# A hybrid diffusion backbone on one core: solve transfers issued by ScalarE, modulation steps paused ahead of the second half's pairs, and six more column pairs in seven products

## The chip, the cores and the metric

The kernel runs on one core of a Trainium2 chip. The time is that of one execution on the device in microseconds (us), as a median over runs. Five engines work side by side, each through its own list of instructions in order: TensorE (PE in the profile; PEld is its weight load), VectorE (DVE), ScalarE (ACT), GpSimd (POOL) and SyncE (SP), which here only issues transfers. A transfer's issue stands in the list of the engine that issues it, and waits there for what it needs.

## The reference, cut to what matters

Two streams of 256 tokens of width 1024, context and latent, go through two layers with the same weights: a SwiGLU FFN at half weight, a mixer, and another FFN. Each of the three parts is modulated by vectors (`mx`, `mc`) that are products of a condition with a large matrix. In the second layer only the latent stream leaves the mixer.

```python
def swiglu(h, w_gu, w_down):
    gate, up = jnp.split(h @ w_gu, 2, axis=-1)
    return (jax.nn.silu(gate) * up) @ w_down
...
    gc = jnp.cumsum(g, axis=-1)                      # gated DeltaNet, chunks of 64
    a = jnp.where(strict, jnp.einsum("bhnid,bhnjd->bhnij", kb, k) * decay, 0.0)
    t = lax.linalg.triangular_solve(eye + a, eye, left_side=True, lower=True, unit_diagonal=True)
    attn = jnp.where(incl, jnp.einsum("bhnid,bhnjd->bhnij", q, k) * decay, 0.0)
...
    for layer in range(DEPTH):
        mx = jnp.split((silu_c @ ada_w[layer] + ada_b[layer])[:, None, :], N_MOD, axis=-1)
        mc = jnp.split((silu_cc @ ada_w[layer] + ada_b[layer])[:, None, :], N_MOD, axis=-1)
        x = x + 0.5 * mx[2] * swiglu(modulate(rmsnorm(x, ...), mx[0], mx[1]), ffn1_wgu, ffn1_wd)
        # cx the same with mc
        fx, gx = mixer_features(hx @ w_in[layer], ...)  # retention q k v, DeltaNet q k v, beta, g, gates
        (ret_c, dn_c), (ret_x, dn_x) = bidirectional_mix(fc, fx, log_gamma)
        x = x + mx[5] * mixer_output(ret_x, dn_x, gx, ...)
        x = x + 0.5 * mx[8] * swiglu(modulate(rmsnorm(x, ...), mx[6], mx[7]), ffn2_wgu, ffn2_wd)
```

The FFN's hidden width is 2816, that is 22 column groups of 128 for the gate and 22 for the up half: a *pair* is a gate group and its up group.

## The kernel before, in words

**Products in three matmuls.** Both streams lie side by side as 512 columns (256 context, 256 latent). Every operand of a large product is kept as a rounded head and a rest: `wh`, `wl` for a weight tile of 128 x 128, `xh`, `xl` for the activations. One tile takes three matmuls of 512 columns, all recorded under line 394 (`mat`). Weights are streamed: SyncE loads 128 x 1024 raw tiles (`_load`, lines 427 and 432), ScalarE rounds the head (`wh`, line 382), VectorE subtracts for the rest (`wl`, line 511). With `self.plo` GpSimd takes every second rest. Four weight tiles make one `wh` and one `wl` of 128 x 512, a group; `_ensure` keeps the heads of the next five groups and the rests of the next four formed, as far as the engines come. A transfer of the next raw tile is issued when the raw buffer before it is freed.

**Pairs in seven products.** `FAST` says how many pairs of an FFN's first and second half go plain; the others of the 11 in a half go through `pairs`, Strassen's scheme over blocks of tiles and of the two streams. It takes seven products of four tiles with 256 columns, 84 matmuls of 256, where a plain pair takes 16 tiles, 48 matmuls of 512. Its weight forms are sums of raw tiles: SyncE loads two more tiles, GpSimd adds by two accumulating transfers (line 461) and two additions (line 464), and seven heads and seven rests are formed instead of four of each. The keys are (layer, FFN), with FFN 0 ahead of the mixer and 2 behind it.

**Modulation steps in the background.** The modulation vectors of all later parts (15 items of 16 steps) are formed by VectorE, one custom row of 128 x 1024 per step (line 803), each on a 512-KB raw tile that SyncE loads two steps ahead (`ada_spread`, line 778). `background` lets a step into VectorE's list whenever `self.gap` microseconds of planned TensorE work have passed; `None` stops them. `RATE` and `RATES` give the gap for plain groups, for pairs and for the down product of an FFN, `MIX_RATE` for the mixers. The first seven items must be done before layer 0's mixing ends.

**FFN.** `ffn` does two halves: 11 pairs, then the down product in eight groups of 11 tiles over this half, each group ending with `evd(m, ...)`, which adds to the residual stream (VectorE, line 388, `s<-mm,mods,s`).

**Mixer.** `run` lets a projection (`dense`) advance while other generators are placed beside it: each yields how much projection work should pass before its next instructions. In layer 0: the retention's keys, queries and values; then `ret_mix` and its gated output beside the other projections; then `dn_small` (the decay `dn_decay`, lengths `dn_len`, scales), `dn_mix` (per chunk set: `dn_prep`) and `dn_scan`. `dn_decay` transposes its 16 inputs (line 398), computes beta and g on VectorE (from line 1523), and has TensorE multiply g with constants (`mx<-g,con`). `dn_prep` forms the system of both directions: transposes of the key and query rows, products of keys and queries, VectorE rows with the decay (line 388, `s<-d,ngc,con`) and products from PSUM (line 385, `s<-mx,s`); then `prep_solve` puts the system to DRAM (`dw`), loads it again as blocks of 16 rows, solves by VectorE subtractions, puts the result to DRAM (`dx`) and loads it as matrices (`ut`). All four kinds of its transfers are issued by SyncE. There are four solves, one for each stream of each layer. The convolution of the DeltaNet's inputs is four VectorE rows of about 508 elements per tile (line 388, `s<-mm,par,s`).

## Time and profile before

| | us |
|---|---|
| median of 3 runs (lowest, highest) | 2405.55 (2404.73, 2806.76) |
| the profiled execution | 2410.67 |
| its span | 2408.9 |
| TensorE busy (matmuls) | 2331.9, 97% |
| VectorE busy | 1762.3, 73% |
| ScalarE busy | 1144.1, 47% |
| GpSimd busy | 549.3, 23% |

The mean granted clock of TensorE in the profiled execution is 0.989 of full speed, whose two levels are 2.4 and 1.2 GHz. The chain of waits that ended last runs through TensorE for 77% of the span, VectorE 12%, issue 5%, DMA 3%, ScalarE 2%. Stretches are named by their start in the profiled execution: layer 0's first FFN ends near 440, its mixer's DeltaNet part starts near 585; layer 1's solves lie near 1880 and 2060.

How to read the views: a *timeline* lists the instructions of one engine in order, with the idle time before each and the last of those it waited for in brackets; *windows* give busy time and granted clock by stretch; *waits* sum the idle time by what ended it; a row *by line* groups instructions of one line and form. For a queue (SPq) a row's duration covers several issues and what stood between them.

### The profile page before, as it was taken

The numbers are of one execution on the slowest core, as the hardware profiler recorded it, in microseconds if no ns is written. First come the engines' busy times: TensorE is split into PE (matmuls) and PEld (weight loads), VectorE is DVE, ScalarE is ACT, GpSimd is POOL, SyncE is SP. The second block draws the span as 40 slices with busy tenths as digits, with TensorE's granted clock in tenths as the row PEclk, the third lists the DMA queues.
The fourth block names the chain that finished last, engine by engine and source line by source line (L and its number), as shares of the span: only waits on it lengthen the run. The fifth ranks groups of instructions, "written<-read, shape, count | busy, mean of one in ns | idle before, by whom it ended". The sixth has DMA issues, their size and how long they took to land.

```text
span 2408.9 us, 42549 instructions
## 1 busy us (share of the span) xinstructions
PE 2331.9 (97%) x16352; PEld 2081.8 (86%) x16352; DVE 1762.3 (73%) x3134; ACT 1144.1 (47%) x2310; POOL 549.3 (23%) x512
## 2 busy tenths in 40 slices
PE   7999999999999999999999999999999899899998
PEld 5888989887788888889899889899888689889998
DVE  6888986558785646579799689899684458677554
ACT  4423545344554444365245365255355446455444
POOL 1003521022330200134144134154124232100001
PEclk9999999999999999999999999999999999999999
DMA  7657763233241414355677555676524324546553
GB/s 287 214 182 221 209 190 121 96 132 132 96 114 58 129 61 149 126 165 143 213 206 193 184 143 155 219 214 183 200 92 138 84 84 138 157 146 222 181 186 112
DMA packets 177325, 377.87 MB, mean 157 GB/s; under 512 B 49697, under 2 KB 54625, under 8 KB 177121
## 3 DMA queue, kind: packets, MB, share of 16 engines
q1 hardware_dynamic: 161184, 346.28, 43.2%
q0 software_dynamic: 13536, 24.65, 6.2%
q10 hardware_dynamic: 2400, 4.23, 0.6%
q8 instruction: 128, 2.10, 0.4%
q14 instruction: 77, 0.62, 0.1%
HBM read 364.83 MB, written 10.26 MB: 156 GB/s over the span
## 4 chain that ended last, share of the span: by engine, by line
PE 77%; DVE 12%; issue 5%; DMA 3%; ACT 2%; SPq 0%; POOL 0%; DVEq 0%; ACTq 0%; POOLq 0%
PE mm L394 66%; PE mx L394 10%; DVE wl L511 5%; DVE s L385 2%; DVE s L803 2%; DVE s L388 2%; ACT s L382 2%; DMA d<-in_adat_dram 1%; PE mx L398 1%; DMA raw<-in_w_dram 0%; ACT wh L382 0%; DVE sub L385 0%; DMA s<-gd 0%; DMA s<-in_x_dram 0%; DVE s L908 0%
## 5 line engine op out<-in xcount | busy, mean ns | idle before, releaser
L394 PE MATMUL mm<-s,wh 128*128 128x256 f32 (+1 forms) x7794 | 1788.4, 324 | 13.0 <-ACT s L382 5.7
L394 PEld LDWEIGHTS mm<-s,wh 128*128 128x128 f32 x7794 | 1295.0, 189 | 142.7 <-ACT s L382 9.0
L394 PE MATMUL mm<-s,wl 128*128 128x256 f32 (+1 forms) x3901 | 1259.0, 323 | 10.6 <-DVE wl L511 8.9
L394 PEld LDWEIGHTS mm<-s,wl 128*128 128x128 f32 x3901 | 738.0, 189 | 73.4 <-DVE wl L511 10.7
L382 ACT ACTIVATE s<-s 128x512 fp32r<-128x512 f32 (+4 forms) x564 | 291.8, 526 | 541.5 <-DVE s L385 287.7
L511 DVE TENSOR_TENSOR wl<-raw,wh 128x512 fp32r<-128x512 f32 x569 | 420.1, 754 | 110.5 <-ACT wh L382 75.5
L382 ACT ACTIVATE wh<-raw 128x512 fp32r<-128x512 f32 x628 | 381.1, 625 | 231.9 <-PE mm L394 140.8
L803 DVE CUSTOM_DVE_ANT_0 s<-d,d,par 128x1024 bf16<-128x1024 f32 x240 | 326.7, 1361 | 33.4 <-DMA d<-in_adat_dram 32.9
L511 DVE TENSOR_TENSOR wl<-s,wh 128x512 fp32r<-128x512 f32 x368 | 311.4, 858 | 21.7 <-ACT wh L382 12.2
L382 ACT ACTIVATE wh<-s 128x512 fp32r<-128x512 f32 x369 | 218.3, 622 | 55.0 <-PE mm L394 46.7
L385 DVE TENSOR_TENSOR s<-s,s 128x512 fp32r<-128x512 f32 (+3 forms) x306 | 191.7, 637 | 40.7 <-ACT s L382 36.8
L382 ACT ACTIVATE s<-mm 128x256 f32<-128x256 f32 (+2 forms) x259 | 110.2, 426 | 228.9 <-PE mm L394 228.5
L464 POOL TENSOR_TENSOR s<-s,raw 128x512 f32<-128x512 f32 x84 | 145.5, 1732 | 111.7 <-DMA raw<-in_w_dram 37.0
L394 PE MATMUL mx<-s,s 32*32 32x32 f32 (+3 forms) x1820 | 152.1, 250 | 11.3 <-DVE s L385 10.1
L394 PEld LDWEIGHTS mx<-s,s 32*32 32x32 f32 (+2 forms) x1820 | 133.6, 149 | 23.2 <-issue 11.5
L461 POOL DMA_DIRECT2D s<-in_w_dram x94 | 83.5, 984 | 277.2 <-DMA s<-in_w_dram 249.5
L908 POOL TENSOR_TENSOR s<-s,s 128x512 f32<-128x512 f32 (+1 forms) x31 | 36.1, 1164 | 435.1 <-ACT s L382 434.8
L511 POOL TENSOR_TENSOR wl<-raw,wh 128x512 fp32r<-128x512 f32 x59 | 80.4, 1363 | 234.9 <-ACT wh L382 113.3
L388 DVE SCALAR_TENSOR_TENSOR s<-mm,mods,s 128x256 f32<-128x256 f32 x132 | 58.7, 478 | 77.5 <-PE mm L394 77.4
L388 DVE SCALAR_TENSOR_TENSOR s<-mm,par,s 128x508 f32<-128x508 f32 (+3 forms) x124 | 87.4, 710 | 13.5 <-ACT s L382 11.1
L385 DVE TENSOR_TENSOR s<-s,mm 128x512 f32<-128x512 f32 (+1 forms) x88 | 54.0, 613 | 42.7 <-PE mm L394 39.5
L382 ACT ACTIVATE s<-mx 128x256 f32<-128x256 f32 (+5 forms) x113 | 50.3, 447 | 72.7 <-PE mx L394 64.3
(227 smaller groups left out, 1528.2 us busy)
## 6 DMA issues: line engine op xcount, KB each, us to landing
raw<-in_w_dram SPq DMA_DIRECT2D x319, 512.0 KB, 3.4
s<-in_w_dram SPq DMA_DIRECT2D x289, 256.0 KB, 5.5
d<-in_adat_dram SPq DMA_DIRECT2D x120, 512.0 KB, 4.7
s<-in_w_dram POOLq DMA_DIRECT2D x94, 256.0 KB, 5.9
s<-in_ada_dram SPq DMA_DIRECT2D x48, 256.0 KB, 5.8
s<-in_tab_dram SPq DMA_DIRECT2D x17, 256.0 KB, 4.5
xd<-s SPq DMA_DIRECT2D x16, 256.0 KB, 4.0
s<-gd ACTq DMA_DIRECT2D x9, 256.0 KB, 6.0
```

The lines of the kernel that those rows point to most:

```text
L382: return self.nc.scalar.activation(out, in_, f, **kw)
L385: return self.nc.vector.tensor_tensor(out, a, b, op)
L388: return self.nc.vector.scalar_tensor_tensor(out, a, s, b, op0=op0, op1=op1)
L394: return self.nc.tensor.matmul(out, lhsT, rhs, start=start, stop=stop, **kw)
L398: return self.nc.tensor.transpose(out, in_, self.ident[:n, :n])
L461: self.nc.gpsimd.dma_start(d[f], b, accum_op=ALU.add)
L464: self.nc.gpsimd.tensor_tensor(d[f], d[src[0]], self.raw[u][0][src[1]], ALU.add)
L511: eng.tensor_tensor(lo, self._src(s), hi.bitcast(F32), ALU.subtract)
L803: self.nc.vector.tensor_tensor_reduce(junk, raw, cb[st], 1.0, self.par[:, b:b + 1], ALU.mult, ALU.add, m[:, st, k:k + 1])
L908: eng.tensor_tensor(acc[:, n0:n1], acc[:, n0:n1], s[:, n0:n1], ALU.add)
```

## The change

Six things differ. `FAST` sends four more pairs of FFN (0, 0) through seven products in its first half, and one more each in (0, 2) and (1, 0). `evd` now sets the gap to `None` also in the first half of those FFNs from group 5 on, so that no step is placed beside the last two down groups; the second half's pairs set it again. `MIX_RATE` becomes 3.0 in layer 0's mixing and 4.0 in layer 1's, and has a third value, 3.6, for layer 0's output stage, which now goes through `run` and so carries steps. In layer 0 `dn_decay` leaves `dn_small` and goes beside `ret_mix`. The transfers of `prep_solve` are issued by ScalarE, with pauses 6, 6, 5 x 2, 1, 6 and 8 for 4, 6, 5 x 2, 5 and 13. In layer 1 GpSimd goes on forming every second rest through the last projections.

```diff
--- before.py
+++ after.py
@@ -61,7 +61,7 @@
 
 
 
-FAST = {(0, 0): (11, 0), (0, 2): (4, 0), (1, 0): (4, 0)}
+FAST = {(0, 0): (7, 0), (0, 2): (3, 0), (1, 0): (3, 0)}
 
 
 def _plain(l, j, half):
@@ -183,7 +183,7 @@
 
 RATE = (10.0, 7.6, 2.2)
 RATES = {(0, 0, 0): (2.8, 8.0, 2.2)}
-MIX_RATE = (2.3, 6.0)
+MIX_RATE = (3.0, 4.0, 3.6)
 
 FIRST_MODS = 7
 
@@ -1189,7 +1189,7 @@
 
             def evd(m, ps, a=n0, b=n1):
                 self.x_add(ps, m, l, gate, a, b)
-                if half == 1 and nxt and m == 3:
+                if half == 1 and nxt and m == 3 or half == 0 and fast and m == 5:
 
                     self.gap = None
                 if half == 1:
@@ -1482,7 +1482,6 @@
                                     self.ph, ALU.pow)
 
         if full:
-            yield from self.dn_decay(l)
             yield lambda: self.nkc == 4
             yield from self.dn_len(self.dk, 0, putk)
         else:
@@ -1721,8 +1720,8 @@
         nc = self.nc
         dw, dx = self.dw, self.dx
         for i, z in enumerate(st):
-            nc.sync.dma_start(dw[i].rearrange("g p n -> p g n"), z["bd"][:, 0:256].rearrange("p (g n) -> p g n", g=8))
-        yield 4.0
+            nc.scalar.dma_start(dw[i].rearrange("g p n -> p g n"), z["bd"][:, 0:256].rearrange("p (g n) -> p g n", g=8))
+        yield 6.0
         ws = self.A()
         W, X = ws[:, 0:256], ws[:, 256:512]
         tmp = self.small([128, 64], "sub", 2)
@@ -1730,7 +1729,7 @@
         part = lambda s, i, f: s[64 * i + 32 * f:64 * i + 32 * f + 32].rearrange("p (r c) -> p r c", r=16)
         for i in range(2):
             for f in range(2):
-                nc.sync.dma_start(part(W, i, f), blk(dw, i, f))
+                nc.scalar.dma_start(part(W, i, f), blk(dw, i, f))
         nc.gpsimd.memset(X, 0.0)
         nc.gpsimd.memset(X[:, 0:256:17], 1.0)
         yield 6.0
@@ -1742,17 +1741,18 @@
             self.tt(xv[:, 0:k, k:16], xv[:, 0:k, k:16], tv, ALU.subtract)
             if k % 3 == 1:
                 yield 2.0
+        yield 1.0
         for i in range(2):
             for f in range(2):
-                nc.sync.dma_start(blk(dx, i, f), part(X, i, f))
+                nc.scalar.dma_start(blk(dx, i, f), part(X, i, f))
         self.Fr(ws)
-        yield 5.0
+        yield 6.0
         for i, z in enumerate(st):
             z["ut"] = ut = self.A()
             for d in range(2):
-                nc.sync.dma_start(ut[:, d * 384:d * 384 + 128].rearrange("p (h n) -> p h n", h=4),
+                nc.scalar.dma_start(ut[:, d * 384:d * 384 + 128].rearrange("p (h n) -> p h n", h=4),
                                   dx[i][d * 4:d * 4 + 4].rearrange("h p n -> p h n"))
-        yield 13.0
+        yield 8.0
 
     def prep_inverse(self, z):
 
@@ -2045,7 +2045,8 @@
             yield from self.gate_out(self.ro, srg, full)
 
         small = self.chain(self.dn_small(l, full), self.dn_mix(l, full))
-        ret = self.chain(self.ret_mix(l, full), ret_out())
+        ret = self.ret_mix(l, full)
+        ret = self.chain(self.zip(ret, self.dn_decay(l)) if full else ret, ret_out())
 
         def d0():
             yield from self.ret_proj_k(full)
@@ -2070,7 +2071,7 @@
 
         def d2v():
             yield from self.dn_proj_v(l)
-            self.plo = False
+            self.plo = not full
 
         if full:
             self.run(d0())
@@ -2093,7 +2094,7 @@
             self.ret = self.gated
             self.run(d2(), self.dn_scan(l, full), scale=0.65)
 
-        self.deep, self.split_dbl = 2, False
+        self.deep, self.split_dbl, self.plo = 2, False, False
         self.bgmax = len(SPREAD)
 
         def d3():
@@ -2132,8 +2133,9 @@
             self.Fr(ys[m])
             y.append(self.split(g, n0, 512, 0.5, 1))
 
-        for _ in self.dense(G_K8, KD, lambda k: dn[k], n0, 512, ev):
-            pass
+        if full:
+            self.gap = MIX_RATE[2]
+        self.run(self.dense(G_K8, KD, lambda k: dn[k], n0, 512, ev))
         for a, b in dn:
             self.Fr(a, b)
         self.sq_start()
@@ -2142,9 +2144,9 @@
             self.x_add(ps, m, l, 5, a, b)
             self.sq_tile(m, a, b)
 
-        for _ in self.dense([4, 1] if full else G_WO, KD, lambda k: y[k], n0, 512, evo):
-            pass
+        self.run(self.dense([4, 1] if full else G_WO, KD, lambda k: y[k], n0, 512, evo))
         if full:
+            self.gap = None
             self.drain()
             for _ in self.tail((5, 6, 7), KD, lambda k: y[k], evo, l, 2):
                 pass
```

What the order of instructions shows at three places. First VectorE, ahead of the first second-half pair of FFN (0, 0): line 803 is a modulation step on the raw tile `d`, `wl<-raw` and `wl<-s` are rests, and line 388 the residual additions of the last two down groups. Before:

```order
L803 ISA s_659,mods<-d_1816,d_658,par 128x1024
L803 ISA mods 128x1
L511 TENSOR_TENSOR wl<-s_1616,wh 128x512
L388 SCALAR_TENSOR_TENSOR s_74<-mm,mods,s_74 128x256 x2
L803 ISA s_659,mods<-d_1859,d_657,par 128x1024
L803 ISA mods 128x1
L511 TENSOR_TENSOR wl<-s_1618,wh 128x512
L803 ISA s_659,mods<-d_1859,d_658,par 128x1024
L803 ISA mods 128x1
L511 TENSOR_TENSOR wl<-s_1770,wh 128x512
```

Of the change:

```order
L803 ISA s_659,mods<-d_1934,d_658,par 128x1024
L803 ISA mods 128x1
L511 TENSOR_TENSOR wl<-raw,wh 128x512
L388 SCALAR_TENSOR_TENSOR s_72<-mm,mods,s_72 128x256 x2
L511 TENSOR_TENSOR wl<-raw,wh 128x512 x3
L388 SCALAR_TENSOR_TENSOR s_73<-mm,mods,s_73 128x256 x2
L511 TENSOR_TENSOR wl<-s_1979,wh 128x512
L511 TENSOR_TENSOR wl<-s_1850,wh 128x512
L388 SCALAR_TENSOR_TENSOR s_74<-mm,mods,s_74 128x256 x2
L511 TENSOR_TENSOR wl<-s_1852,wh 128x512
L803 ISA s_659,mods<-d_1975,d_657,par 128x1024
L803 ISA mods 128x1
```

Before, a step stands ahead of nearly every rest, those of the pair's first forms (`wl<-s`) among them; now none stands from the residual addition of `s_72` to the third of these rests.

Then VectorE, in layer 0's `dn_prep` for the context, from the decay rows (`ngc,con`) to the last product of the system (`s<-mx,s`), which reads the PSUM buffer of the key products. Before:

```order
L388 SCALAR_TENSOR_TENSOR s_6500<-d_6452,ngc,con 128x128 x4
L511 TENSOR_TENSOR wl<-raw,wh 128x512
L388 SCALAR_TENSOR_TENSOR s_6447<-mm,par,s_6447 128x2x255
L388 SCALAR_TENSOR_TENSOR s_6447<-mm,par,s_6447 128x2x254
L388 SCALAR_TENSOR_TENSOR s_6532<-mm,par,s_6532 128x2x254
L388 SCALAR_TENSOR_TENSOR s_6532<-mm,par,s_6532 128x2x255
L385 TENSOR_TENSOR s_6578<-mx,s_6478 128x512
L385 TENSOR_TENSOR s_6582<-mx,s_6484 128x512
L511 TENSOR_TENSOR wl<-raw,wh 128x512
L388 SCALAR_TENSOR_TENSOR s_6532<-mm,par,s_6532 128x2x255
L388 SCALAR_TENSOR_TENSOR s_6532<-mm,par,s_6532 128x2x254
L385 TENSOR_TENSOR s_6607<-mx,s_6489 128x512
```

Of the change:

```order
L388 SCALAR_TENSOR_TENSOR s_6770<-mm,par,s_6770 128x2x254
L388 SCALAR_TENSOR_TENSOR s_6770<-mm,par,s_6770 128x2x255
L803 ISA s_659,mods<-d_6658,d_658,par 128x1024
L803 ISA mods 128x1
L385 TENSOR_TENSOR s_6820<-mx,s_6716 128x512
L385 TENSOR_TENSOR s_6824<-mx,s_6722 128x512
L511 TENSOR_TENSOR wl<-raw,wh 128x512
L388 SCALAR_TENSOR_TENSOR s_6770<-mm,par,s_6770 128x2x255
L388 SCALAR_TENSOR_TENSOR s_6770<-mm,par,s_6770 128x2x254
L803 ISA s_659,mods<-d_6772,d_657,par 128x1024
L803 ISA mods 128x1
L385 TENSOR_TENSOR s_6852<-mx,s_6727 128x512
```

Steps of line 803 now stand between the convolution rows (`mm,par`) and the system's products; before, the last step of the mixing stood ahead of all of these.

Last ScalarE, in layer 1's latent solve. Before, SyncE's queue held the solve's transfers (lines 1724 and 1733, later 1747 and 1753) among the weight loads:

```order
L1724 DMA dw_190<-s_21658 128x8x32
L1724 DMA dw_191<-s_21664 128x8x32
L427 DMA raw<-in_w_dram 128x1024
L2022 DMA yd_18535<-s_21873 128x256
L1733 DMA d_21924<-dw_190 32x16x16 x2
L1733 DMA d_21924<-dw_191 32x16x16 x2
L427 DMA raw<-in_w_dram 128x1024 x2
L2022 DMA yd_18535<-d_21924 128x256
L427 DMA raw<-in_w_dram 128x1024 x2
```

Of the change, ScalarE's list holds them among the heads:

```order
L1723 DMA dw_190<-s_22039 128x8x32
L1723 DMA dw_191<-s_22045 128x8x32
L382 ACTIVATE wh<-raw 128x512 x3
L1732 DMA s_22322<-dw_190 32x16x16 x2
L1732 DMA s_22322<-dw_191 32x16x16 x2
L382 ACTIVATE wh<-raw 128x512
L382 ACTIVATE s_22352<-mm 128x256
L382 ACTIVATE wh<-raw 128x512 x4
L382 ACTIVATE s_22464<-mm 128x256
L382 ACTIVATE wh<-raw 128x512 x2
L382 ACTIVATE s_22511<-mm 128x256
L382 ACTIVATE wh<-raw 128x512 x2
```

The weight loads no longer have a solve's transfer ahead of them in their queue, and the heads (`wh`) now have.

## Rows read from the trace of the kernel before

**Rows 1.** Timeline of TensorE, second-half pair starts: start, duration, engine, line, operation, [idle before <-releaser].
```profile
221.45 0.58 PE L394 MATMUL mm<-s,wl 128*128 128x256 f32 x1 [2.40 <-DVE wl L511]
...
1216.80 0.39 PE L394 MATMUL mm<-s,wl 128*128 128x256 f32 x1 [1.75 <-DVE wl L511]
...
1575.23 0.39 PE L394 MATMUL mm<-s,wl 128*128 128x256 f32 x1 [1.17 <-DVE wl L511]
```
**Rows 2.** Windows of TensorE: stretch, length, busy (matmuls), granted clock, DMA share, GB/s.
```profile
222.00:226.00 4.00, 4.00 (x26) 0.67 0.42 75
608.00:612.00 4.00, 3.89 (x12) 0.50 0.00 0
1218.00:1222.00 4.00, 4.00 (x23) 0.59 0.51 155
```
**Rows 3.** Timeline of TensorE, layer 0's mixing, the decay.
```profile
585.07 0.42 PE L398 MATMUL mx<-con,s 16*128 16x16 f32 x4
...
608.11 1.01 PE L394 MATMUL mx<-g,con 128*128 128x16 f32 x4 [11.38 <-issue]
```
**Rows 4.** Timeline of SyncE's queue, layer 1's context solve.
```profile
1830.14 46.23 SPq L427 DMA_DIRECT2D raw<-in_w_dram  x12
1876.42 1.05 SPq L1724 DMA_DIRECT2D dw<-s  x2
...
1882.55 13.28 SPq L427 DMA_DIRECT2D raw<-in_w_dram  x2
1895.88 2.04 SPq L1747 DMA_DIRECT2D dx<-s  x4
1899.78 2.03 SPq L1753 DMA_DIRECT2D s<-dx  x4
```
**Rows 5.** Line 385, VectorE, plain pairs: operation xcount: duration min/median/max, first to last start.
```profile
L385 DVE TENSOR_TENSOR s<-s,mm x3: 687/689/689, 119.2 to 141.2; 128x512 f32<-128x512 f32 x3
```
**Rows 6.** Line 1133, GpSimd, pairs by seven products (columns as above).
```profile
L1133 POOL TENSOR_TENSOR s<-s,s x9: 731/735/741, 238.6 to 321.1; 128x256 f32<-128x256 f32 x9
```
**Rows 7.** Timeline of VectorE, ahead of the first second-half start.
```profile
213.55 1.29 DVE L803 CUSTOM_DVE_ANT_0 s<-d,d,par 128x1024 bf16<-128x1024 f32 x1 [2.98 <-DMA d<-in_adat_dram]
...
219.65 1.74 DVE L511 TENSOR_TENSOR wl<-s,wh 128x512 fp32r<-128x512 f32 x1
```
**Rows 8.** Waits of TensorE, the first first-half start: total us, times, longest.
```profile
PE mm L394 <- DVE s L385: 1.0, 1, 1.0
```
**Rows 9.** Timeline of VectorE, the copy of the decay's inputs.
```profile
597.91 0.22 DVE L1523 COPY bt<-mx 128x64 f32<-128x64 f32 x1
```
**Rows 10.** VectorE by line, 560 to 600 us: shapes xcount, busy us, mean ns, idle before.
```profile
L803 DVE CUSTOM_DVE_ANT_0 s<-d,d,par 128x1024 bf16<-128x1024 f32 x11 | 15.1, 1377 | 0.0
L388 DVE SCALAR_TENSOR_TENSOR s<-mm,par,s 128x508 f32<-128x508 f32 (+1 forms) x14 | 10.4, 742 | 0.2
L385 DVE TENSOR_TENSOR s<-s,s 128x512 fp32r<-128x512 f32 x8 | 7.1, 883 | 0.8 <-ACT s L382 0.7
L385 DVE TENSOR_TENSOR s<-mx,s 128x512 f32<-128x512 f32 x8 | 5.5, 683 | 0.0
L511 DVE TENSOR_TENSOR wl<-raw,wh 128x512 fp32r<-128x512 f32 x4 | 2.7, 681 | 0.0
```
**Rows 11.** VectorE by line, 640 to 700 us, the decay rows.
```profile
L388 DVE SCALAR_TENSOR_TENSOR s<-d,ngc,con 128x128 f32<-128x128 f32 x16 | 7.8, 556 | 1.6 <-DMA d<-gd 1.5
```
**Rows 12.** Timeline of VectorE, layer 1's context solve.
```profile
1874.27 0.31 DVE L1672 STREAM_TRANSPOSE s<-s 128x128 f32<-128x128 f32 x1
...
1894.61 0.17 DVE L385 TENSOR_TENSOR s<-s,sub 128x15 f32<-128x15 f32 x1
```
**Rows 13.** Waits of TensorE, layer 1's latent solve.
```profile
PE mm L394 <- DVE wl L511: 3.6, 3, 1.5
PE mx L394 <- DVE s L385: 2.2, 1, 2.2
```
**Rows 14.** Timeline of GpSimd, ahead of the first second-half start.
```profile
217.35 3.50 POOL L464 TENSOR_TENSOR s<-s,raw 128x512 f32<-128x512 f32 x2 [11.13 <-DVE wl L511]
```

## The prediction

> **What bounds the kernel now.** I read the page first: TensorE is busy for 97% of the span (the table above), so a saving counts only where it shortens TensorE's own work or one of the few stretches in which it stands. Then I read the timeline of TensorE around each place that the diff touches, the windows behind each stand (they show the granted clock), and the timelines of VectorE, SyncE and GpSimd that say who was late. The reader is to see three kinds of loss. At the start of the column pairs in the second half of three FFNs, TensorE waits for a weight rest [rows 1] and then runs below full clock [rows 2]. In layer 0's mixing it stands 11.38 us before the product with the cumulative decay g [rows 3]. In layer 1's two triangular solves the small transfers stand in SyncE's queue behind weight loads [rows 4], and weight loads behind them.
>
> **Six more pairs by seven products.** Three plain pairs are two intervals of 11.0 us apart; nine rows that stand once in each seven-product pair are eight intervals of (321.1 - 238.6) / 8 = 10.3 us [rows 5, 6]. So a pair saves 0.7 us, six save 4.2, and up to 6 where the small waits of the second form are hidden. I take **-4.5**. Each such pair brings two GpSimd adds of 1.75 us and its accumulating transfers, beside TensorE; that cover has its price in the third rival.
>
> **Modulation steps paused before the second half's pairs.** The new condition stops the steps for the last two of the eight down groups. Before, VectorE takes the rests in order behind modulation steps, and a step waits for its own 512-KB load: 2.98 us at 213.55 [rows 7]. TensorE then waits 2.40, 1.75 and 1.17 us at the three starts [rows 1], and the first two are followed by four microseconds at clock 0.67 and 0.59, which is (1 - 0.67) x 4 = 1.3 and (1 - 0.59) x 4 = 1.6 us of work lost [rows 2]. In the order of the change the rests stand there without a step between them, so VectorE can be several rests ahead. I take all five back: **-8.2**. The least is -3 (third rival).
>
> **A new start of pairs in the first half of FFN (0, 0).** It has steps at a gap of 2.8 us before it and no pause. The two first-half starts that exist wait about a microsecond or less (1.0 at the first) [rows 8]; the worst second-half start cost 2.40 + 1.3 = 3.7 [rows 1, 2]. I take **+1.5**, nearer to its own kind, with ends 0 and +3.7.
>
> **The decay moved into the retention.** The transposes of the decay's inputs ran at 585.07 [rows 3], VectorE came to their copy at 597.91 [rows 9], 12.4 us behind, and TensorE needed g 11.38 us before it was there. Four microseconds at clock 0.50 follow [rows 2], another 2.0. In the new order far more projection work stands between the two, so **-13.4** comes back.
>
> But VectorE's backlog does not go away; what is late next? It was made of VectorE's work outrunning TensorE's: in the 62 rows before the copy there are 14 convolution rows, 13 modulation steps and 22 full-width ones, some 45 us by the means of [rows 10], beside 12 groups of four weight tiles (GpSimd forms every second rest) at a quarter of a plain pair each [rows 5], 33 us; the difference, 12, is the lag seen. The seventh set of steps, which must end in this mixing, ended before the solve's inputs were formed; with the gap of 3.0 it ends after. In the new order the stretch from the row of the query lengths to the last product of the system holds 14 convolution rows (10.4), six steps (6 x 1.37 = 8.2), the sixteen decay rows (7.8), eight full-width rows (8 x 0.68 = 5.4) and ten small ones (about 1): 32.8 us by [rows 10, 11]. TensorE has there 96 matmuls of 512 columns at 11.0 / 48 = 0.229 and 28 small ones at 10.3 / 84 = 0.12 us [rows 5, 6]: 25.4 us. The same sum over the 62 rows ahead gives 42 us (28 convolution rows, 12 steps, 7 rests) against 14 groups, 38.5, so VectorE comes in some 3.5 us late. At the end of the stretch TensorE wants a PSUM buffer that the last product of the system frees: it would stand 3.5 + 32.8 - 25.4 = 11 us, and lose 2.0 at half clock as it does now. I take **+13**, with 0 (the first rival) and +22 (VectorE comes in with the old lag of 12.4 instead of 3.5) as ends.
>
> **The solves' transfers by ScalarE, with other pauses.** In layer 1's context solve the input is ready at 1874.27 + 0.31, its transfer leaves at 1876.42; the result is ready at 1894.61 + 0.17, its transfer leaves at 1895.88 behind two loads that held SyncE from 1882.55 for 13.28 us [rows 4, 12]. That is 1.9 + 1.1 = 3.0 us late, and I take 2 of it. In the latent solve TensorE waits 3.6 us in three pieces for weight rests and 2.2 for the solve [rows 13]; the loads stand there behind the solve's transfers. I take 4 of 5.8. Together **-6**, ends -9 and 0. Layer 0's two solves have wide groups beside them and TensorE does not stand there; I cost them at 0. If their cover goes, the fourth rival is the price. The Trainium skill, page "DMA: Bandwidth & Descriptors", section "Issuing engines are not separate DMA queues", says that transfers started by several engines run on the same 16 DMA engines and that another issuer saves only the issue time. By it this term would be about 0 and the time the second rival's. The rows here speak of another thing: 13.28 us in which SyncE waited with a load at its head, and that is not issue time.
>
> **Small edits.** The gap of 4.0 for 6.0 in layer 1, the eleven steps in layer 0's output stage at 3.6, and GpSimd's odd rests in layer 1's last projections lie beside TensorE where it is busy throughout. I cost them at 0, ends -2 and +3 (the worst wait of [rows 1] once).
>
> **Sum.** -4.5 - 8.2 + 1.5 - 13.4 + 13 - 6 = -17.6. The profiled execution would go from 2410.67 to 2393; it lies 5.1 above the median of the runs, 2405.55, and from that comes **2388 us**.
>
> **The rivals.**
> *First, VectorE keeps up in the solve's inputs* and no new stand takes g's place: -17.6 - 13 = -30.6, 2375 us. For it: the stand is a small difference of sums of 75 and 64 us. Against: the same sum gives the old lag within 0.5 us.
> *Second, the solve transfers gain nothing by ScalarE*, since it now stands for them in order and its weight heads come as late as the loads did: the term -6 is 0, 2394 us.
> *Third, the pair starts keep most of their waits.* GpSimd's two adds took 3.50 us together [rows 14], and VectorE's rest beside them 1.74 us [rows 7] where one takes 0.68 [rows 10]. Where that slows the rests, not the steps, the pause gives 3 of 8.2 us: 2393 us. The Trainium skill, page "SBUF — State Buffer", section "Who interferes with whom", says that VectorE with two SBUF inputs and GpSimd share a port pair, of which one holds the other off; the row of 1.74 agrees.
> *Fourth, the other side:* ScalarE stands in all four solves from the first transfer until the last has left, 1876.42 to 1901.81 [rows 4], 25.4 us, and forms no weight heads meanwhile. The code forms the heads of five groups ahead: 5 x 2.75 = 13.8 us in three solves, half that in the last with its 256 columns. The full price is 3 x 11.6 + 18.5 = 53 us; it decides as soon as ScalarE waits longer than 13.8 us in one piece. In the order weight heads stand between the transfers, so at most half of it: +26 on the gain without the -6, 2388 + 6 + 26 = 2420, slower than before.
>
> **Chances.** Forecast 0.42, first rival 0.22, second 0.12, third 0.10, fourth 0.07, the rest, neither of these, 0.07. The range reaches from the first rival with the pairs at -6 and the solves at -9 (2375 - 4.5 = 2370) and a little further for the new start and the small edits (-1.5 and -2, and what the sums are rounded by), to the second and third together (2399) with the new stand at its worst (+9): **2364 to 2408**. This kernel's measurement can tell about 2%, 48 us, from no change; the first rival does not reach that and the fourth only at its full price. Faster by over 2%: 0.05, within 2%: 0.93, slower: 0.02.
>
> **What would show it.** In the changed profile the GpSimd row of the seven-product pairs should stand 53 times, at 10.3 us; the three second-half starts should have no wait for a rest over 0.5 us. The wait before g should be gone, and a wait of about 11 us on VectorE stand at the query-key products of layer 0's context solve, with clock 0.5 behind it: none there means the first rival. ScalarE should wait at most 4 us for a solve's transfer; over 13.8, the fourth. The forecast is wrong if the time leaves the range, or if it holds with these signs absent.

## The result: slower by 1.1%, where 0.7% faster was forecast

The changed kernel takes 2433.95 us (median of 4 runs, 2430.89 to 2437.43), the kernel before 2406.78 in the four runs beside it: a ratio of 1.0112 (95% interval 1.0099 to 1.0124). One of these four took 2806.76 us, a slow run, and is left out of the ratio. The forecast was 2388 us in a range of 2364 to 2408. The profiled execution took 2435.14 us. The page of the changed kernel:

```profile
span 2433.4 us, 43193 instructions
...
PE 2338.1 (96%) x16568; PEld 2093.9 (86%) x16568; DVE 1789.9 (74%) x3135; ACT 1158.8 (48%) x2346; POOL 625.8 (26%) x571
...
PE 68%; DVE 19%; issue 5%; ACT 3%; DMA 3%; POOL 0%; ACTq 0%; SPq 0%; DVEq 0%; POOLq 0%
```

TensorE is busy 6 us longer in a span that is 24.5 us longer. So it stands for 18 of the 24.5 us, and behind the stands it runs below full clock. To see where, cut both traces at the same rows of VectorE's residual additions (line 388, `s<-mm,mods,s`, 132 of them in each trace, in the same order; the differences of their starts):

| stretch (from row to row of the 132) | before | after | difference |
|---|---|---|---|
| FFN (0, 0), first half's pairs (start to 1) | 159.9 | 162.2 | +2.3 |
| FFN (0, 0), its first down product and second half (1 to 29) | 222.1 | 217.9 | -4.2 |
| layer 0's mixer (29 to 33) | 619.9 | 632.5 | **+12.6** |
| FFN (0, 2), first half's pairs (33 to 49) | 161.4 | 165.8 | +4.4 |
| FFN (0, 2), second half (49 to 77) | 221.7 | 218.7 | -3.0 |
| FFN (1, 0), first half's pairs (77 to 81) | 139.4 | 145.5 | +6.1 |
| FFN (1, 0), second half (81 to 105) | 205.9 | 204.6 | -1.3 |
| layer 1's mixer (105 to 109) | 457.5 | 465.0 | **+7.5** |

These sum to +24.4. Each is from one execution, and stretches of the same code differ between the executions on record. With the old pair table the first stretch took 158.8 to 162.9 us in seven of them, FFN (0, 2)'s first half 159.6 to 163.1 in six and FFN (1, 0)'s 139.3 to 140.0. So the +2.3 alone shows nothing. The +4.4 and +6.1 lie outside: seven executions with the new table and the head of the change took 165.8 to 168.0 and 144.3 to 146.3.

**The three second-half starts** did what was forecast. Where [rows 1] had waits of 2.40, 1.75 and 1.17 us, the windows of TensorE (columns as in [rows 2]) show it busy at full clock, idle for 0.2 us at most:

```profile
205.00:230.00 25.00, 24.83 (x166) 1.00 0.78 217
1220.00:1240.00 20.00, 19.80 (x149) 1.00 0.62 171
1584.00:1604.00 20.00, 20.00 (x156) 1.00 0.56 164
```

The second half of FFN (0, 0) tells the pause from the new pairs: it took 216.8 to 218.2 us in all twelve executions with the pause, whichever the table, and 221.0 to 222.5 in the four without it, one of them with the new table (run 6).

**The three first-half starts** have a wait of 3 to 4 us each, at the third of the first pair's seven products, and clock below full behind it (a window of 4 us is a mean over the two levels). Timeline and windows of TensorE:

```profile
115.10 0.51 PE L394 MATMUL mm<-s,wh 128*128 128x256 f32 x2 [3.32 <-ACT s L382]
...
1081.83 0.51 PE L394 MATMUL mm<-s,wh 128*128 128x256 f32 x2 [3.21 <-ACT s L382]
...
1445.20 0.80 PE L394 MATMUL mm<-s,wh 128*128 128x256 f32 x2 [4.34 <-ACT s L382]
```

```profile
116.00:120.00 4.00, 4.00 (x23) 0.57 0.40 87
1082.00:1086.00 4.00, 4.00 (x22) 0.57 0.97 166
1444.00:1448.00 4.00, 2.80 (x13) 0.53 0.95 266
1448.00:1452.00 4.00, 4.00 (x24) 0.62 0.20 76
```

What TensorE waits for is ScalarE's copy of the first sum out of PSUM, where TensorE adds up its products (1081.41, done at 1081.77), since the third product adds to the same buffer. Timelines of VectorE and ScalarE at the second start:

```profile
1078.43 1.29 DVE L385 TENSOR_TENSOR s<-s,s 128x512 fp32r<-128x512 f32 x2
1079.64 0.68 DVE L385 TENSOR_TENSOR s<-s,mm 128x512 f32<-128x512 f32 x1
```

```profile
1080.35 0.63 ACT L382 ACTIVATE s<-s 128x512 fp32r<-128x512 f32 x1 [2.93 <-DVE s L385]
...
1081.41 0.36 ACT L382 ACTIVATE s<-mm 128x256 f32<-128x256 f32 x1
```

Read from the end: the copy stands behind a head (1080.35), which waited 2.93 us for VectorE's multiply (1079.64), the last of the plain pairs'; and VectorE came to it behind the rests of the transformed inputs (1078.43). An engine that works in order passed one late row on to two others.

**Layer 0's mixer.** The wait for g of [rows 3] is gone, five others stand in its place, three of them of 4.2 to 4.6 us. The waits (total us, times, longest) and windows of TensorE and VectorE from 580 to 730 us (windows: TensorE busy, weight loads, VectorE, ScalarE, GpSimd, clock, DMA share, GB/s):

```profile
PE mx L398 <- POOL s L1399: 5.4, 2, 4.2
PE mx L394 <- ACT s L382: 4.8, 2, 4.2
PE mx L394 <- DVE d L385: 4.6, 1, 4.6
```

```profile
580.00:640.00 60.00, 59.43 (x264) 45.11 (x262) 59.36 (x90) 31.40 (x55) 18.79 (x13) 1.00 0.43 149
640.00:680.00 40.00, 34.58 (x168) 28.61 (x167) 39.26 (x72) 21.06 (x45) 20.07 (x13) 0.96 0.37 121
680.00:730.00 50.00, 40.57 (x390) 32.03 (x390) 37.86 (x81) 17.16 (x35) 14.95 (x26) 0.86 0.50 135
```

VectorE is busy for 59.4 of 60 and 39.3 of 40 us, and for 37.9 of the next 50. The same windows of before, where the wait for g gave it air:

```profile
580.00:640.00 60.00, 48.62 (x215) 37.38 (x214) 48.79 (x94) 29.07 (x53) 14.46 (x10) 0.89 0.26 90
640.00:680.00 40.00, 40.00 (x206) 33.47 (x205) 31.73 (x62) 27.86 (x56) 21.39 (x16) 1.00 0.28 91
680.00:730.00 50.00, 49.72 (x582) 40.48 (x581) 36.02 (x85) 22.53 (x52) 12.71 (x26) 1.00 0.49 130
```

The clock of TensorE behind the stands (columns as in [rows 2]):

```profile
664.00:668.00 4.00, 2.85 (x17) 0.75 0.40 161
668.00:672.00 4.00, 4.00 (x16) 0.82 0.41 127
692.00:696.00 4.00, 4.00 (x14) 0.50 0.17 68
720.00:724.00 4.00, 1.02 (x77) 0.58 0.44 109
724.00:728.00 4.00, 4.00 (x78) 0.57 0.70 236
```

The reason lies in VectorE's rows of line 803, the modulation steps. Of before (count, duration min/median/max in ns, first and last start):

```profile
L803 DVE CUSTOM_DVE_ANT_0 s<-d,d,par x34: 1274/1276/1284, 67.8 to 157.1; 128x1024 bf16<-128x1024 f32 x34
...
L803 DVE CUSTOM_DVE_ANT_0 s<-d,d,par x13: 1271/1276/2375, 558.8 to 609.5; 128x1024 bf16<-128x1024 f32 x13
```

Of after:

```profile
L803 DVE CUSTOM_DVE_ANT_0 s<-d,d,par x24: 1272/1278/2372, 68.6 to 158.4; 128x1024 bf16<-128x1024 f32 x24
...
L803 DVE CUSTOM_DVE_ANT_0 s<-d,d,par x21: 1272/1276/2383, 559.0 to 638.0; 128x1024 bf16<-128x1024 f32 x21
...
L803 DVE CUSTOM_DVE_ANT_0 s<-d,d,par x13: 1273/1275/2293, 641.3 to 707.0; 128x1024 bf16<-128x1024 f32 x13
```

In 440 to 560 us there are 18 before and 14 after; the steps at 558.8 and 559.0 reach over 560 us and are counted in both stretches. So 47 steps instead of 30 lie in the mixing: 17 steps of 1.37 us, 23 us of VectorE's time. 13 now stand after 640 us, beside the forming of the solve's inputs, where before there was none. Ten of them are missing in FFN (0, 0)'s first half, where plain groups take a step every 2.8 us of work and seven-product pairs one every 8.0; seven in its second half, where the pause stands. That the pairs leave VectorE no room for more shows a window of before in the second half's pairs, with VectorE busy for 39.37 of 40 us (columns as in the windows from 580 us):

```profile
240.00:280.00 40.00, 38.91 (x322) 38.31 (x321) 39.37 (x54) 22.86 (x47) 23.17 (x20) 1.00 0.80 209
```

**The solves on ScalarE.** Its timeline in layer 0's and layer 1's context solve shows it standing in front of the transfer of the result, with weight heads behind it:

```profile
714.14 0.63 ACT L382 ACTIVATE wh<-raw 128x512 fp32r<-128x512 f32 x1 [11.75 <-issue]
...
1915.93 1.15 ACT L382 ACTIVATE wh<-raw 128x512 fp32r<-128x512 f32 x2 [13.67 <-issue]
```

**Layer 1's mixer.** GpSimd's rests (line 511) and VectorE's subtractions of the solves by line, 1818 to 2135 us:

```profile
L511 POOL TENSOR_TENSOR wl<-raw,wh 128x512 fp32r<-128x512 f32 x58 | 78.8, 1360 | 133.7 <-ACT wh L382 91.0 <-PE mm L394 31.8 <-PE mx L394 10.7
```

```profile
L511 DVE TENSOR_TENSOR wl<-raw,wh 128x512 fp32r<-128x512 f32 x58 | 50.5, 875 | 40.0 <-ACT wh L382 36.8 <-DMA dx<-s 3.0
...
L385 DVE TENSOR_TENSOR sub<-s 128x15 f32<-128x15 f32 (+7 forms) x30 | 9.4, 313 | 9.3 <-DMA s<-dw 8.5
...
L385 DVE TENSOR_TENSOR s<-s,sub 128x15 f32<-128x15 f32 (+7 forms) x30 | 8.3, 276 | 1.0
```

```profile
PE mx L394 <- DVE s L385: 6.7, 1, 6.7
PE mx L394 <- DVE d L385: 5.0, 1, 5.0
PE mm L394 <- POOL wl L511: 4.0, 2, 2.2
```

The wait for the latent solve is 5.0 us where [rows 13] had 2.2, and two waits of together 4.0 us end with a rest of GpSimd's, where before one did, of 1.7 us. The wait for the context solve is 6.7; before it was 7.0, the longest of this row:

```profile
PE mx L394 <- DVE s L385: 9.2, 2, 7.0
```

### The profile page after: what moved, and what is told of

It is laid out like the page before. It is cut to its first block, busy times and chain, and to the rows that moved or that the text cites. A ratio compares the mean times of both kernels' runs of the same rounds, so it can differ in the third digit from the quotient of the medians.

```text
span 2433.4 us, 43193 instructions
## 1 busy us (share of the span) xinstructions
PE 2338.1 (96%) x16568; PEld 2093.9 (86%) x16568; DVE 1789.9 (74%) x3135; ACT 1158.8 (48%) x2346; POOL 625.8 (26%) x571
## 4 chain that ended last, share of the span: by engine, by line
PE 68%; DVE 19%; issue 5%; ACT 3%; DMA 3%; POOL 0%; ACTq 0%; SPq 0%; DVEq 0%; POOLq 0%
PE mm L394 58%; PE mx L394 9%; DVE wl L511 6%; DVE s L385 4%; DVE s L803 4%; DVE s L388 3%; ACT s L382 2%; ACT wh L382 1%; DMA raw<-in_w_dram 1%; DMA s<-in_ada_dram 1%; PE mx L398 0%; DVE sub L385 0%; DMA s<-in_w_dram 0%; DMA d<-in_adat_dram 0%; DMA s<-dw 0%
## 5 line engine op out<-in xcount | busy, mean ns | idle before, releaser
L394 PEld LDWEIGHTS mm<-s,wh 128*128 128x128 f32 x7938 | 1314.8, 190 | 147.7 <-ACT s L382 21.8
L394 PEld LDWEIGHTS mm<-s,wl 128*128 128x128 f32 x3973 | 754.1, 190 | 66.9 <-DVE wl L511 5.0
L511 DVE TENSOR_TENSOR wl<-raw,wh 128x512 fp32r<-128x512 f32 x538 | 397.6, 753 | 112.6 <-ACT wh L382 76.7
L511 DVE TENSOR_TENSOR wl<-s,wh 128x512 fp32r<-128x512 f32 x388 | 338.0, 883 | 21.0 <-ACT wh L382 12.0
L382 ACT ACTIVATE s<-mm 128x256 f32<-128x256 f32 (+3 forms) x264 | 110.1, 417 | 224.9 <-PE mm L394 218.8
L511 POOL TENSOR_TENSOR wl<-raw,wh 128x512 fp32r<-128x512 f32 x88 | 121.0, 1376 | 296.4 <-ACT wh L382 145.2
L464 POOL TENSOR_TENSOR s<-s,raw 128x512 f32<-128x512 f32 x92 | 158.1, 1718 | 84.6 <-DMA raw<-in_w_dram 45.6
L394 PE MATMUL mx<-s,s 32*32 32x32 f32 (+3 forms) x1792 | 148.7, 251 | 14.8 <-DVE s L385 8.9
L1133 POOL TENSOR_TENSOR s<-s,s 128x256 f32<-128x256 f32 x53 | 41.3, 779 | 242.9 <-ACT s L382 239.4
L394 PE MATMUL mm<-s,s 128*128 128x256 f32 (+1 forms) x624 | 83.2, 291 | 4.9 <-DVE s L385 3.5
```

Of the source, the lines that this page charges most:

```text
L382: return self.nc.scalar.activation(out, in_, f, **kw)
L394: return self.nc.tensor.matmul(out, lhsT, rhs, start=start, stop=stop, **kw)
L464: self.nc.gpsimd.tensor_tensor(d[f], d[src[0]], self.raw[u][0][src[1]], ALU.add)
L511: eng.tensor_tensor(lo, self._src(s), hi.bitcast(F32), ALU.subtract)
L1133: self.nc.gpsimd.tensor_tensor(g[:, rc], g[:, rc], c[:, lc], ALU.mult)
```

## The experiments

Each ran beside the kernel before on the same chip, whose medians there were 2407 to 2408 us. All but three start from the changed kernel, 2434 us.

**1. The old pair table in the changed kernel.**

```diff
-FAST = {(0, 0): (7, 0), (0, 2): (3, 0), (1, 0): (3, 0)}
+FAST = {(0, 0): (11, 0), (0, 2): (4, 0), (1, 0): (4, 0)}
```


> The changed kernel with the old pair table: 11, 4 and 4 plain pairs ahead of the first half's seven-product pairs, all other parts of the change kept. Theory A (the new or earlier starts of pairs in the first halves cost more than the pairs save): between the residual additions of the FFNs' down products the changed kernel lost 2.3, 4.5 and 7.6 us against the kernel before in the three first halves, so these 14.4 us come back: about 2420 us. Rival (the starts are harmless, a seven-product pair saves 0.7 us each): 4.5 us are lost, about 2438 us.

2399.01 us, ratio to before 0.9961 (0.9946 to 0.9975): 35 us came back, not 14. The first halves of the FFNs (0, 2) and (1, 0) gave 5.9 each, the 12 expected; FFN (0, 0) gave nothing in its own stretch (162.9 us for 162.2), but layer 0's mixer went from 632.5 to 615.6 us and layer 1's from 465.0 to 459.6. The rest of the change without the pairs is a gain.

**2. The head ahead of the pairs formed later.** In `ev`:

```diff
+                    if fast and half == 0 and m == 2 * _plain(l, j, 0) - 1:
+                        hid.append(self.split(s, n0, n1, 2, 3))
+                    else:
+                        hid.append(self.split(s, n0, n1, 0, 1))
```


> The changed kernel, but the head of the last plain pair's hidden tile (ScalarE) is formed two groups later, so that it no longer stands ahead of the copy of the first seven-product sum out of PSUM. Theory A (TensorE waits at the third product for that copy, which stands on ScalarE behind a head that waits for VectorE's multiply): the waits of 3.3, 3.2 and 4.3 us and the half clock behind them (about 1.7 us each) go: 12 to 16 us less, 2418 to 2422 us. Rival (the transformed inputs or the weight forms are late in themselves): TensorE waits there as long, for another row: 2431 to 2437 us.

2424.88 us, 1.0077 (1.0062 to 1.0092): 9 of 12 to 16 us. The waits of TensorE from 1068 to 1098 us:

```profile
PE mm L394 <- ACT s L382: 1.0, 1, 1.0
```

The wait of 3.2 us for ScalarE's copy is down to 1.0: the cause was the order on ScalarE. The three first halves are 2.1, 3.3 and 4.4 us shorter. VectorE is still late, so smaller waits for weight rests are left.

**3. The solves' transfers back on SyncE**, all four kinds, with the old pauses.

```diff
-            nc.scalar.dma_start(dw[i]...)
+            nc.sync.dma_start(dw[i]...)
```


> The changed kernel with the solves' transfers issued by SyncE again and the old pauses. Theory S (ScalarE stands 11.8, 13.7 and 6.4 us for the solves' results and TensorE pays for it): the wait of 4.6 us and the half clock at layer 0's context solve (3.4 us) and part of the 5.0 us at layer 1's latent solve go: about 10 us less, 2424 us. Rival (VectorE is late there anyway, and GpSimd's rests slow its subtractions): no change, 2434 us within 3.

2430.23 us, 1.0098 (1.0081 to 1.0115): 4 us less by the medians, between the two, but the interval overlaps that of the change (1.0099 to 1.0124). In the profiled execution layer 0's mixer lost 4.1 us of its 12.6 and layer 1's 2.0 of its 7.5. The stands of [rows 4] were not what bounded these stretches.

**4. Modulation steps from the mixer's start.**

```diff
         def d0():
+            if full:
+                self.gap = MIX_RATE[l]
             yield from self.ret_proj_k(full)
```


> The changed kernel, but layer 0's mixing carries modulation steps at the gap of 3.0 from its start, through the retention's key, query and value projections, where VectorE is 35 to 60% busy; the seventh item then ends before the DeltaNet part. Theory B (VectorE's backlog of steps makes the waits of 1.2, 4.2 and 4.2 us in layer 0's solve, and the half clock behind them, about 5 us): these go, and 12 to 15 us come back: 2419 to 2422 us; what is left there is the wait of 4.6 us for the solve's result. Rival (the waits come from ScalarE's and GpSimd's order, not from the steps): 2434 us within 3.

2421.13 us, 1.0061 (1.0044 to 1.0078), 13 us less: theory B. All steps of the first seven items now begin before 535 us, and TensorE's waits and windows of the stretch that lost most are:

```profile
PE mx L394 <- DVE d L385: 1.1, 1, 1.1
```

```profile
580.00:640.00 60.00, 60.00 (x281) 47.14 (x280) 44.47 (x65) 31.25 (x56) 17.38 (x12) 1.00 0.26 91
640.00:680.00 40.00, 40.00 (x205) 33.35 (x204) 31.61 (x61) 26.14 (x53) 21.04 (x16) 1.00 0.26 89
680.00:730.00 50.00, 48.89 (x579) 39.72 (x577) 36.04 (x84) 23.68 (x54) 13.17 (x26) 1.00 0.46 127
```

It is busy for 148.9 of the 150 us, where it was 134.6. The mixer as a whole gained only 10.8 us (632.5 to 621.7), since the early steps brought a new wait: TensorE stands 5.04 us until 448.49, for VectorE's rows of the retention (line 385), which come behind the steps; it was not a wait for weights.

**5. The old table in FFN (0, 0) alone.**

```diff
-FAST = {(0, 0): (7, 0), (0, 2): (3, 0), (1, 0): (3, 0)}
+FAST = {(0, 0): (11, 0), (0, 2): (3, 0), (1, 0): (3, 0)}
```


> The changed kernel with 11 plain pairs in FFN (0, 0)'s first half again; the other two FFNs keep 3. Theory B (the four pairs there keep VectorE full, so that some 17 modulation steps are pushed into layer 0's mixing, where TensorE then waits): the mixing's loss of 16.9 us comes back, FFN (0, 0) itself changes by under 1 us, the starts in the other two FFNs (4.5 and 7.6 us) stay: about 2417 us. Rival (the mixing's waits come from the moved decay and ScalarE's transfers): 2432 to 2438 us.

2408.24 us, 0.9999 (0.9990 to 1.0009): 26 us less, more than expected: 15.7 in layer 0's mixer, 1.2 in the FFN itself, 4.9 in layer 1's mixer. There are 10 steps fewer in the mixing (37 instead of 47), all of them after 640 us, where 3 stand instead of 13:

```profile
L803 DVE CUSTOM_DVE_ANT_0 s<-d,d,par x3: 1273/1276/1277, 640.8 to 650.3; 128x1024 bf16<-128x1024 f32 x3
```

From 580 to 680 us VectorE is as full as in the change (59.4 of 60 and 39.0 of 40 us), and from 680 to 730 it is busy for 28.9 instead of 37.9. This points to how long VectorE's backlog lasts, more than to its being full.

**6. The new pair table in the kernel before.**

```diff
-FAST = {(0, 0): (11, 0), (0, 2): (4, 0), (1, 0): (4, 0)}
+FAST = {(0, 0): (7, 0), (0, 2): (3, 0), (1, 0): (3, 0)}
```


> The kernel before with the new pair table alone (7, 3 and 3 plain pairs). Theory A and B together (starts 14.4 us, pushed steps some 17 us, less nothing for the pairs, whose saving is already in the 14.4): about 2407 + 31 = 2438 us. Rival (a seven-product pair saves 0.7 us wherever it stands, the losses need the other parts of the change): 2402 us.

2418.63 us, 1.0046 (1.0031 to 1.0061): neither. The starts cost about what was expected (+4.0, +4.4 and +5.7 us in the first halves), but the mixer only 0.8: the wait of 11.37 us for g still stands, and VectorE can work off the ten pushed steps in it and in the air behind it. So the pushed steps cost time only together with the other parts of the change; with which of them was not tried one by one.

**7. The moved decay in the kernel before.**

```diff
-            yield from self.dn_decay(l)
             yield lambda: self.nkc == 4
...
-        ret = self.chain(self.ret_mix(l, full), ret_out())
+        ret = self.ret_mix(l, full)
+        ret = self.chain(self.zip(ret, self.dn_decay(l)) if full else ret, ret_out())
```


> The kernel before with the decay moved beside the retention alone. Theory C (the wait of 11.4 us for g and the half clock behind it go, and VectorE's backlog gives part of it back at the solve): 2407 - 13.4 + 6 = about 2400 us. Rival (the backlog moves on in full): 2407 within 3. Other rival (VectorE catches up): 2394 us.

2403.43 us, 0.998 (0.997 to 0.9989), a gain of 4.6 us, between theory C and the rival that the backlog moves on in full; in the mixer of the profiled execution only 1.5 (619.9 to 618.4). TensorE's timeline shows the wait for g at another place, and one for the lengths where it used to be:

```profile
521.14 0.59 PE L394 MATMUL mx<-g,con 128*128 128x16 f32 x4 [3.02 <-ACT wh L382]
...
606.18 1.66 PE L394 MATMUL mx<-s,ones 128*32 128x512 f32 x4 [2.30 <-ACT s L382]
```

The view names rows of ScalarE, but VectorE is behind both: its last row of g ends at 521.12, just ahead of the product, and from 598 to 611 us it has no idle time. The 11.38 us of [rows 3] were for the most part not the price of an order but of VectorE's backlog; what needs VectorE next pays it.

**8. No rests by GpSimd in layer 1's last projections.**

```diff
-            self.plo = not full
+            self.plo = False
```


> The changed kernel without GpSimd's every second rest in layer 1's last projections. Theory P (GpSimd's rests beside VectorE's subtractions, 0.38 us each where they took 0.20, and its wait of 2.2 us, make the latent solve later): 3 to 5 us less, 2430 us. Rival (VectorE would be later with all the rests): 2434 to 2438 us.

2425.54 us, 1.0075 (1.0060 to 1.0091), 8 us less. Layer 1's mixer takes 458.5 us, 6.5 less. GpSimd's rests and VectorE's subtractions there, by line:

```profile
L511 POOL TENSOR_TENSOR wl<-raw,wh 128x512 fp32r<-128x512 f32 x30 | 39.6, 1322 | 78.0 <-ACT wh L382 43.0 <-PE mm L394 18.6 <-PE mx L394 16.3
```

```profile
L385 DVE TENSOR_TENSOR sub<-s 128x15 f32<-128x15 f32 (+7 forms) x30 | 7.3, 242 | 9.4 <-DMA s<-dw 8.7
L385 DVE TENSOR_TENSOR s<-s,sub 128x15 f32<-128x15 f32 (+7 forms) x30 | 6.2, 207 | 1.0
```

One takes 242 and 207 ns on average, where it took 313 and 276 beside 58 of GpSimd's rests instead of 30. But the 6.5 us are the price with the whole change. Runs 1, 5 and 9, which keep these rests, have this mixer at 459.6, 460.1 and 460.8 us, and run 11, which is run 1 with early steps and without the rests, at 457.2. In the change seven modulation steps begin in this mixer and in runs 1, 5 and 9 none, which fits; no run tried it.

**9. The old gap of 2.3 in layer 0's mixing.** `MIX_RATE = (2.3, 4.0, 3.6)`.

> The changed kernel with layer 0's mixing at the old gap of 2.3 instead of 3.0. The seventh item of modulation steps then ends just ahead of the rows of the solve's inputs, not 90 rows behind them. Theory B1 (what matters is that steps stand between the solve's inputs and its result): the waits of 4.2 and 4.2 us and one of the two stretches at half clock go, about 2424 us. Theory B2 (what matters is VectorE's whole backlog, whichever rows make it): the waits move ahead, 2434 us within 3.

2425.16 us, 1.0077 (1.0054 to 1.0101): 9 us, near B1; 5.7 of them in the mixer. The waits moved ahead (3.2 us for g near 520, 2.6 for the lengths near 605) and got smaller. So both hold in part. That the same backlog costs less where no solve waits behind it fits this, but was not shown apart.

**10. The old table, the solves on SyncE and no rests by GpSimd in layer 1** (the edits of 1, 3 and 8 together).

> The changed kernel with the old pair table, the solves' transfers on SyncE with the old pauses, and no rests by GpSimd in layer 1's last projections: what is left of the change is the pause ahead of the second half's pairs, the moved decay and the gaps. If the gains of the single edits add up: 2399 - 4 - 8 = 2387 us. Rival (layer 1's loss was there only with the steps and pairs of the full change): 2396 to 2399 us.

2395.36 us, **0.9948 (0.9929 to 0.9968)**: faster than both kernels, though 4 and 8 us do not add to what run 1 had won. Layer 0's mixer takes 612.9 us, 7.0 less than before.

**11. The old table, early steps, no rests by GpSimd in layer 1** (1, 4 and 8 together).

> The changed kernel with the old pair table, steps from the start of layer 0's mixing, and no rests by GpSimd in layer 1's last projections. Theory B: with the old table the backlog is small already, so the early steps give little here and cost the waits for weights that they brought at the mixer's start (5 us); the rests give some 8: 2391 to 2396 us.

2395.91 us, 0.9951 (0.9934 to 0.9967), as expected; the mixer takes 618.7 us, 3.1 more than in run 1: there is little backlog to mend, and the early steps bring their own wait (5.05 us until 448.50).

**12. All six pairs with the mends** (2, 4 and 8 together).

> As the run before, but with the six more pairs and the later head ahead of them. It differs from that run by the six pairs with two of their three side costs taken away. If a seven-product pair saves 0.7 us once its start and the pushed steps are mended, it comes out 0 to 4 us below that run's time; if the multiply ahead of the pairs stays late and the pairs keep VectorE full, 5 to 12 us above it: about 2404 us. I expect the second.

2405.96 us, 1.0002 (0.9988 to 1.0015): 10 us above run 11, as expected. The first halves of (0, 2) and (1, 0) are 5.1 and 2.8 us longer than there.

**13. The same with four plain pairs again in (0, 2) and (1, 0).**

> As the run with the six pairs and all mends, but with 4 plain pairs again in the FFNs (0, 2) and (1, 0); the four pairs of FFN (0, 0) stay, with the later head and with early steps to take what they push away. Theory D (the four pairs pay their 2.8 us once the steps have another place; the fourth plain pair of the other two was the cover of their transformed inputs): 5 to 8 us below that run, and 0 to 3 us below the run with the old table: 2393 to 2398 us, to 2396 with the old table. Rival (the four cost as much inside FFN (0, 0) as they save): the same as the old table, 2396 to 2400 us.

2402.81 us, 0.9979 (0.9969 to 0.9989): missed, 7 us above run 11. The first half of FFN (0, 0) is 2.6 us shorter (162.2 to 159.6), what four pairs at 0.7 should give, but the 2.6 us lie ahead of the pairs. From VectorE's first multiply of a plain pair (60.4 us in run 11, 57.7 here) to the first residual addition it takes 101.8 us there and 101.9 here. So the four pairs give nothing in all: TensorE still waits 1.4 and 1.2 us for VectorE at their start. FFN (0, 2)'s first half is 3.7 us longer than in run 11, but run 10, with the old table and no later head, has 163.1 us as well. In both the granted clock falls ahead of the pairs (0.91 from 1000 to 1020 us in run 10; 0.95 and 0.96 from 1000 to 1040 here; 1.00 in run 11). Where the rest of the 7 us lies is not settled.

**14. The solves on ScalarE in the kernel before** (the edit of 3, the other way).

> The kernel before with the solves' transfers on ScalarE and the new pauses alone. My term in the prediction: 6 us less, 2402 us. The rule that another issuer gains nothing: 2408. Theory S (ScalarE stands for the solves' results and the heads come late, some 4 us as the kernel with SyncE again showed): 2410 to 2413 us.

2410.61 us, 1.0006 (0.9994 to 1.0018): no difference that can be told, so the term of -6 is 0 by itself. Layer 1's mixer stayed at 457.3 us (457.5), layer 0's went up by 3.2.

## Why the prediction was wrong, step by step

Its sum was -17.6; the stretches give +24.4. Term by term:

- *Pause ahead of the second halves, -8.2:* right, in size and in mechanism; -4.2, -3.0 and -1.3 in the stretches that hold these starts, and the waits are gone.
- *Six pairs, -4.5, and one new start, +1.5:* the first halves give +12.8 (2.3, 4.4, 6.1). The step that failed is that I counted one new start. In the FFNs (0, 2) and (1, 0) the pair that became a seven-product pair was the last plain one, under which VectorE and ScalarE formed the transformed inputs; that cover was never named. [rows 8] misled me: the wait of 1.0 us there is at the end of the first wide group, and the pair starts of before, which had four plain pairs ahead, have no wait. Run 2 shows the mechanism, runs 1 and 6 the price. Nor did a run get back the saving of 0.7 us a pair that [rows 5, 6] promise: between the same two rows four pairs of FFN (0, 0) took as long as four plain ones even with the later head (101.9 and 101.8 us, runs 13 and 11).
- *The moved decay, -13.4, and the new stand, +13:* together -0.4, measured +12.6 for the mixer. The mechanism was the one forecast (VectorE full, TensorE waiting at the solve's inputs, half clock behind) but the size was not. The step that failed here is the size of VectorE's backlog. The stands of 5.4, 4.8 and 4.6 us and the five windows at clock 0.50 to 0.82, in which some 6 us of work are lost, make about 20, not 13; some 6 us of the +12.6 lie outside these rows and are not accounted for. Run 5 shows that 15.7 us hang on the pairs of FFN (0, 0), which push 10 steps into the mixing, behind 640 us: I counted the steps in the solve's stretch, and not what the new pairs, which keep VectorE full, take from the FFN. The same pairs in the kernel before cost the mixer only 0.8 us (run 6), so it takes both, the pushed steps and another part of the change; which part is open. And the gain was hardly one by itself: run 7 got 1.5 us of 13.4 in the mixer, 4.6 in the time.
- *The solves on ScalarE, -6:* 0 by itself (run 14). With the rest of the change run 3 puts it at +4 by the medians, not clear of their intervals, and at 4.1 and 2.0 us in the two mixers. The fourth rival had the mechanism, a ScalarE that stands in order, but at the wrong place and price. The queue wait of 13.28 us in [rows 4] was real, and freeing it changed little: TensorE waits there for the solve's chain, 6.7 us where it was 7.0. The Trainium skill (page "DMA: Bandwidth & Descriptors", section "Issuing engines are not separate DMA queues") says that another issuer saves only the time of the issue; run 14 (a ratio of 1.0006) agrees with that, and not with my argument against it.
- *Small edits, 0:* GpSimd's rests in layer 1 cost 6.5 us of its mixer with the rest of the change (run 8), and with the old pair table about 2 (runs 1 and 11: 459.6 and 457.2 us), so the pairs have a part in the +7.5 as well. I had a row for it, 1.74 for 0.68 us beside GpSimd [rows 7, 10], and used it for another place. The Trainium skill (page "SBUF — State Buffer", section "Who interferes with whom") says that a VectorE instruction with two SBUF inputs contends with a GpSimd instruction that reads SBUF; the slower subtractions (276 ns, and 207 in run 8) fit it.

Of the signs named, three came (53 rows of the seven-product pairs; no wait at the second-half starts; no wait of 11 us for g). The wait at the solve came larger, 14.8 us in five pieces, and ScalarE stood 11.75 and 13.67 us where I had allowed 4; the fourth rival's mark was 13.8, and its price of 26 us did not come (run 3).

## What to carry to other kernels

A wait that ends with an engine that is always busy can be that engine's backlog: then moving what waits moves the wait (run 7). Before work is taken from the bounding engine, ask what it was the cover for, on every engine that ran beneath it, and where the background work that filled those gaps will go. An issue put on an in-order engine waits there with everything behind it, 11.75 and 13.67 us here. A stretch of one execution is no proof of a saving of 2 or 3 us: look for the same code in other executions first.

## What the runs showed of the hardware

Behind each of the six stands of TensorE of 3 to 5 us whose windows are shown, one or two windows of 4 us have a mean clock of 0.50 to 0.82; the work lost in them is 1.4 to 2.8 us a stand. The second subtraction of a step of the solves on VectorE took 207 ns on average in run 8, and 276 in the change, with 58 of GpSimd's subtractions in the stretch instead of 30.
